# Halving the moving operand of one group of matmuls: the gate products of the second channel mixer in a two-layer decoder trunk

## The chip, the cores and the metric

One Trainium2 chip; the program runs on one core. The metric is device time in microseconds of one execution, as a median over runs. TensorE (PE, with its weight loads shown apart as PEld), VectorE (DVE), ScalarE (ACT), GpSimd (POOL) and SyncE (SP, which issues the large DMAs) run side by side and meet through semaphores.

## The reference

A decoder trunk of two layers over 256 tokens with a width of 2048. The first layer mixes tokens by sparse attention, the second by stick-breaking attention on a shared K/V; each is followed by a channel mixer, and every branch is normalised, shifted and scaled by a conditioning vector. What the change touches is the channel mixer of the second layer (`layer = 1`, `D_FF = 5632`):

```python
def swiglu(h, w_in, w_out):
    gate, up = jnp.split(h @ w_in, 2, axis=-1)
    return (jax.nn.silu(gate) * up) @ w_out

for layer in range(2):
    ...
    h = modulate(rms_norm(x, norm_g[layer, 2]), sh2, sc2)
    y = swiglu(h, ffn_w_in[layer], ffn_w_out[layer])
    x = x + g2[:, None, :] * rms_norm(y, norm_g[layer, 3])
```

All inputs are float32, and `h @ w_in` has 256 x 2048 by 2048 x 11264 elements; the left half of the result is the gate, the right half is up.

## The kernel before

**Tiling.** A weight matrix is cut into blocks of 512 columns (`nb`), and each block into four pieces of 512 rows (`kt`). One piece is one DMA of 1 MB into a page `raw` of 128 partitions x 2048 (four chunks `j` of 128 rows, 512 columns each). ScalarE rounds it into a page `wh` of type float32r, and VectorE subtracts to get the remainder `wl`. The activations are split in the same way into `hh` and `hl`; they lie transposed, in one page per `kt` (called `hhF` in the profile for the channel mixers). The 256 tokens are two tiles `t` of 128.

**The products.** For every chunk `j`, `piece` issues three matmuls into one PSUM bank `acc` of 128 x 512 float32: `hh` by `wh`, `hh` by `wl`, `hl` by `wh`. The 128 x 128 tile of activations is the stationary operand, and the 128 x 512 chunk of weights is the moving one, so that each matmul brings a weight load of its own (an LDWEIGHTS row in the profile, of the activations). The profile's names read out<-moving,stationary: `acc<-wh,hhF` is the first and the third of the three, `acc<-wl,hhF` the second.

**The channel mixer.** `ffn_units(l, key, ...)` has 11 blocks of 512 gate columns (segment `"g0"` in the first layer, `"g1"` in the second) and 11 of up columns (`"u0"`, `"u1"`), alternately: gate block, up block, next gate block. One block is 4 `kt` x 2 `t` x 4 `j` x 3 = 96 matmuls. After six blocks comes a part of the output product (`"p1"`), then the other five blocks, then the rest (`"y1"`). When a gate block is done, ScalarE takes its silu (`sg`), VectorE multiplies by up, and TensorE transposes the result (`aT`), between later products.

**What sets the order.** The whole program is written out by a planner (`Emit`) that runs while the program is built. It keeps a clock per engine and adds the cost that `_cost` gives each instruction; by these clocks it decides when a weight piece is split, which of the waiting side jobs (transposes, softmax, modulation vectors) comes between two products, which page or bank a tile gets, and how many filler matmuls (`idle<-identb`, bf16, 256 columns, results unused) `fill` puts ahead of a matmul that it expects to wait. A changed cost can therefore change the order. `_cost` gives a matmul with a float32r moving operand of `n` columns `n / 2400 + 0.0133` us. Besides the products above, the `gate_unit` of the first layer has 48 float32r matmuls of 256 columns (`gacc`, stationary `wh` or `wl` of 48 columns).

Every engine call goes through the helper `Engine.call`, so all instructions have its line in the profile: L118 before, L119 in the changed kernel.

Of the kernel before, what the change touches and what calls it, by code (L numbers as in the profile page):

```python
# [10 lines left out]
R32 = mybir.dt.float32r  # L11
# [14 lines left out]
NB = 512  # L26
# [33 lines left out]
FILL_LEAVE = 0.7  # L60
LEADS = (5.0, 5.0, 5.0)
M_FFN = 80

C_ID, C_NTRI, C_ANY, C_NEG1, C_ONE, C_KEEP = 0, 128, 256, 258, 259, 260
C_MASK, C_MASKT, C_CMP, C_COS, C_SIN, C_END = 260, 388, 516, 548, 804, 1060
# [32 lines left out]
class Engine:  # L98
# [5 lines left out]
    def __getattr__(self, op):  # L104
        f = getattr(self.real, op)
        E, eng = self.E, self.name

        def call(*a, **k):
            acc = k.get("accum_out")
            aps = [v for v in list(a) + [v for n, v in k.items() if n != "accum_out"] if hasattr(v, "free_size")]  # L110
            out, ins = aps[0], aps[1:]
            load = 0.0
            if eng == "ACT" and a[2] in TABLES and TABLES[a[2]] != E.table:
                E.table, load = TABLES[a[2]], 1.28
            if eng == "PE":
                E.fill(aps)
            E.enter(eng, _cost(eng, op, out, ins, k, acc), [out] + ([acc] if acc is not None else []), ins, load)
            return f(*a, **k)  # L118

        return call  # L120


def _cost(eng, op, out, ins, k, acc):
    n = out.free_size()
    if eng == "PE":
        if op == "transpose":
            return 0.109
        if ins[1].dtype != F32:
            return max(n / 2400.0 + 0.0133, 0.04)
        if out.shape[0] <= 64 and n >= 128:  # L130
            return n / 2400.0 + 0.09 if out.shape[0] <= 32 else n * 2 / 2400.0 + 0.02
        return 2 * max(n * 2 / 2400.0 + 0.0133, 0.109)
    n = max([n] + [i.free_size() for i in ins])
    if eng == "ACT":
        ptr = sum(hasattr(k.get(x), "free_size") for x in ("bias", "scale")) + (acc is not None)
        return 0.08 + n * 0.000833 + 0.093 * ptr
    if eng == "DMA2":
        return 3.0
    if eng == "DMA":
        return n * 4 * P / 383e3  # L140
    fast = op in ("tensor_scalar", "tensor_copy") and out.space == ins[0].space and list(ins[0].ap)[-1][0] == 1
    ptr = 0.055 * (op in ("tensor_scalar", "scalar_tensor_tensor"))
    return 0.075 + ptr + n / (1920.0 if fast else 960.0)
# [308 lines left out]
def kernel(ctx: ExitStack, tc, consts, x, c, mod_w, mod_b, norm_g, ffn_w_in, ffn_w_out, a_w_in,  # L452
# [9 lines left out]
    V, A, T, DMA = E.V, E.A, E.T, E.D  # L462
# [1142 lines left out]
    def mods_of(vecs):  # L1605
        return [("mod", v, k) for v in vecs for k in range(16)]
# [3 lines left out]
    def keys_of(a, b):  # L1610
        ks = []
        for u in units[a:b]:
            k = u.get("key")
            if k and k not in seen:
                seen.add(k)
                ks.append(k)
        return ks
# [4 lines left out]
    def spread(ks, mods, tail, head=0):  # L1622


        tot = sum(cost(k) for k in ks[head:len(ks) - tail])
        o, m, c = [], 0, 0.0
        for i, k in enumerate(ks):
            if i >= head:
                c += cost(k)
            want = min(len(mods), round(len(mods) * c / tot))  # L1630
            while m < want:
                o.append(mods[m])
                m += 1
            o.append(k)
        return o
# [22 lines left out]
    m1 = mods_of([(0, 5), (2, 1), (2, 0), (1, 1), (1, 0)])  # L1658
    order += spread(keys_of(n_l0, n_f0), m1[:M_FFN], TAIL, HEAD)
    order += spread(keys_of(n_f0, n_l1), m1[M_FFN:] + mods_of([(1, 2), (1, 4), (1, 3)]), TAIL, HEAD)  # L1660
    order += spread(keys_of(n_l1, len(units)), mods_of([(1, 5)]), 20, HEAD)
# [33 lines left out]
    def release(u, i):  # L1695
        if last_use[u["key"]] == i:
            del E.ready[u["key"]]
            E.put("pg")
            if u["key"][0] != "w1":
                E.put("pg")  # L1700
        if u["kind"] == "mm" and last_lhs[u["lhs"]] == i:
            E.put("pg")

    def weights(key):
        return E.ready[key][2] if key in E.ready else None

    def bank(tag):
        return E.when_free(tag)

    def latest(*ts):  # L1710
        return None if any(x is None for x in ts) else max(ts)

    def mm_unit(i, u):
        t, lhs = u["t"], u["lhs"]

        def start_time():
            return latest(weights(u["key"]), E.flags.get(u.get("flag", (lhs[0], lhs[1], t))),
                          bank(u["tag"]) if u["start"] else 0.0)

        js = u.get("js", range(4))  # L1720

        def piece(j):
            if u["start"] and j == 0:
                accs[u["acc"]] = E.alloc(u["tag"], "acc")
            wh, wl, _ = E.ready[u["key"]]
            o = accs[u["acc"]]
            hh = L[lhs][:, 0, j, t * P:(t + 1) * P]
            hl = L[lhs][:, 1, j, t * P:(t + 1) * P]
            T.matmul(o, hh, wh[:, j], start=u["start"] and j == 0, stop=False)
            T.matmul(o, hh, wl[:, j], start=False, stop=False)  # L1730
            T.matmul(o, hl, wh[:, j], start=False, stop=u["stop"] and j == 3)
            if j == js[-1]:
                if u["stop"]:
                    first = u["acc"][0] in ("g0", "g1", "kv") and u["nb"] == 0 and t == 0
                    E.spawn(after(u["epi"](accs.pop(u["acc"]), t, u["nb"]), E.fin + 0.1, first), front=True)
                release(u, i)

        return Unit(u["key"], start_time, [lambda j=j: piece(j) for j in js])

    def after(gen, t, calm=False):  # L1740
        yield t
        while calm and E.urgent:
            yield False
        yield from gen
# [73 lines left out]
```

## Time and profile before

| what | value |
|---|---|
| time, median of 3 runs | 2411.55 us (2410.32 to 2412.08) |
| the profiled execution, first to last instruction | 2407.8 us (its whole time is not listed; the median is 3.75 us above this) |
| mean granted TensorE clock | 0.996 |
| PE busy, PEld busy | 2356.9 us (98%), 1906.6 us (79%) |
| DVE busy, ACT busy | 1633.4 us (68%), 1077.6 us (45%) |
| HBM traffic | 272 GB/s over the span |

The busy time of PE is a union of intervals whose ends are modelled, and neighbouring matmuls overlap in the record; the distance between the starts of two matmuls tells more than the duration of one. In the rows of the timeline, equal neighbours are merged: the first number is the start, the second the length from the first start to the last end, and xN the count.

### The profile page before, as it was taken

Reading aid. Unit: us, or ns where it says so; the run is one execution under the profiler, and the core shown is the slowest. Engines: PE = TensorE matmul, PEld = TensorE weight load, DVE = VectorE, ACT = ScalarE, POOL = GpSimd, SP = SyncE. Lnnn points to the kernel's source line nnn. Section 1 sums busy time; section 2 is a strip of 40 time slices with the busy share of each in tenths; the row PEclk is TensorE's granted clock in tenths of the full one; section 3 lists DMA queues with packets and bytes.
Section 4 is the critical chain, followed back from the end, with each engine's and each line's share of the span. In section 5 each row is a group of like instructions: output and inputs, shape, how many; then the busy total and the mean of one; then the engine's idle time right before and its main releaser. Section 6 shows DMA issues by size and latency. Waiting matters only on the chain.

```text
span 2407.8 us, 27188 instructions
## 1 busy us (share of the span) xinstructions
PE 2356.9 (98%) x11124; PEld 1906.6 (79%) x11124; DVE 1633.4 (68%) x1346; ACT 1077.6 (45%) x1217; POOL 5.6 (0%) x14
## 2 busy tenths in 40 slices
PE   6999999999999999999999999999999999999998
PEld 4677777877888888888877788887888888888886
DVE  3788789978766667767768778865645454554554
ACT  4343455563433333333455455765433333333342
POOL 0000000000000000000000000000000000000000
PEclk9999999999999999999999999999999999999999
DMA  9998967979887699878758979845756547855642
GB/s 350 389 388 281 354 245 250 362 252 397 283 309 273 224 330 399 327 273 307 260 197 333 339 272 399 315 166 196 269 191 220 200 152 244 304 193 196 221 160 105
DMA packets 265629, 657.54 MB, mean 273 GB/s; under 512 B 12449, under 2 KB 30113, under 8 KB 240161
## 3 DMA queue, kind: packets, MB, share of 16 engines
q1 hardware_dynamic: 263808, 649.13, 75.0%
q0 software_dynamic: 992, 6.32, 0.7%
q8 instruction: 87, 1.43, 0.2%
q10 hardware_dynamic: 704, 0.36, 0.1%
q14 instruction: 38, 0.30, 0.0%
HBM read 653.64 MB, written 2.13 MB: 272 GB/s over the span
## 4 chain that ended last, share of the span: by engine, by line
PE 86%; ACT 4%; DMA 4%; DVE 3%; SPq 1%; issue 1%; ACTq 0%; DVEq 0%
PE acc L118 78%; DMA raw<-in_a_w_in_dram 2%; PE sc L118 1%; SPq L118 1%; DVE wl L118 1%; PE oT L118 1%; PE z L118 1%; ACT wh L118 1%; ACT hf L118 1%; ACT junk L118 1%; PE aT L118 1%; DMA modw<-in_mod_w_dram 1%; PE pmod L118 1%; DMA modq<-in_mod_w_dram 1%; PE hT L118 1%
## 5 line engine op out<-in xcount | busy, mean ns | idle before, releaser
L118 DVE TENSOR_TENSOR wl<-raw,wh 128x2048 fp32r<-128x2048 f32 (+2 forms) x392 | 880.0, 2249 | 516.9 <-ACT wh L118 477.8
L118 ACT ACTIVATE wh<-raw 128x2048 fp32r<-128x2048 f32 (+2 forms) x392 | 734.6, 1880 | 683.5 <-PE acc L118 478.7
L118 PE MATMUL acc<-wh,hhF 128*128 128x512 f32 x2816 | 883.7, 392 | 0.0
L118 PEld LDWEIGHTS acc<-wh,hhF 128*128 128x128 f32 x2816 | 530.4, 188 | 113.7 <-issue 4.2
L118 PE MATMUL acc<-wl,hhF 128*128 128x512 f32 x1408 | 549.3, 390 | 0.0
L118 DVE SCALAR_TENSOR_TENSOR macc<-modw,cact,macc 128x2048 f32<-128x2048 f32 x180 | 422.5, 2347 | 38.1 <-DMA modw<-in_mod_w_dram 29.2
L118 PE MATMUL acc<-wh,fa 128*128 128x512 f32 x1408 | 437.4, 390 | 0.0
L118 PEld LDWEIGHTS acc<-wh,fa 128*128 128x128 f32 x1408 | 264.3, 188 | 55.8 <-issue 0.8
L118 PEld LDWEIGHTS acc<-wl,hhF 128*128 128x128 f32 x1408 | 265.4, 188 | 53.8
L118 PE MATMUL acc<-wl,fa 128*128 128x512 f32 x704 | 273.9, 389 | 0.0
L118 PE MATMUL acc<-wh,hA 128*128 128x512 f32 x640 | 220.7, 404 | 1.4 <-DVE hA L118 0.7
L118 PE MATMUL acc<-wh,hhK 128*128 128x512 f32 x512 | 161.4, 392 | 0.9 <-ACT wh L118 0.7
L118 PEld LDWEIGHTS acc<-wl,fa 128*128 128x128 f32 x704 | 132.2, 188 | 26.9
L118 PEld LDWEIGHTS acc<-wh,hA 128*128 128x128 f32 x640 | 120.1, 188 | 39.7 <-issue 15.0
L118 PE MATMUL acc<-wl,hA 128*128 128x512 f32 x320 | 125.4, 392 | 3.0 <-DVE wl L118 3.0
L118 PEld LDWEIGHTS acc<-wh,hhK 128*128 128x128 f32 x512 | 96.0, 188 | 22.6 <-ACT wh L118 1.1
L118 PE MATMUL acc<-wl,hhK 128*128 128x512 f32 x256 | 100.3, 392 | 1.2 <-DVE wl L118 1.2
L118 ACT ACTIVATE fa<-aT 128x512 fp32r<-128x512 f32 x44 | 26.0, 594 | 162.8 <-PE aT L118 150.6
L118 PE MATMUL acc<-wh,hhB 128*128 128x512 f32 x256 | 87.5, 401 | 0.0
L118 PE MATMUL acc<-wh,oA 128*128 128x512 f32 x256 | 84.8, 398 | 0.0
L118 PE MATMUL acc<-wh,oB 128*128 128x512 f32 x256 | 82.4, 394 | 0.0
L118 PEld LDWEIGHTS acc<-wl,hA 128*128 128x128 f32 x320 | 60.4, 189 | 13.6 <-DVE wl L118 4.2
(183 smaller groups left out, 1664.9 us busy)
## 6 DMA issues: line engine op xcount, KB each, us to landing
raw<-in_ffn_w_in_dram SPq DMA_DIRECT2D x176, 1024.0 KB, 5.3
modw<-in_mod_w_dram SPq DMA_DIRECT2D x160, 1024.0 KB, 7.1
raw<-in_ffn_w_out_dram SPq DMA_DIRECT2D x88, 1024.0 KB, 5.3
raw<-in_a_w_in_dram SPq DMA_DIRECT2D x40, 1024.0 KB, 14.2
modq<-in_mod_w_dram SPq DMA_DIRECT2D x32, 1024.0 KB, 14.1
modw<-in_kv_mod_w_dram SPq DMA_DIRECT2D x32, 1024.0 KB, 5.7
raw<-in_kv_w_dram SPq DMA_DIRECT2D x32, 1024.0 KB, 7.6
raw<-in_a_w_out_dram SPq DMA_DIRECT2D x16, 1024.0 KB, 7.1
```

Source lines behind the costliest of these rows:

```text
L118: return f(*a, **k)
```

## The change

In `piece`, the gate products of the second layer (`"g1"` alone) are issued as two matmuls of 256 columns each instead of one of 512, for each of the three products. Both halves have the same stationary tile and go to the two halves of the same bank. The accumulation of the bank is started by the first half alone. The planner's cost of a float32r matmul of exactly 256 columns becomes `256 * 17 / 16 / 2400` = 0.1133 us, from 0.1200 us; a matmul of 512 columns stays at 0.2266 us. This cost also holds for the 48 `gacc` matmuls of the first layer, whose form is not changed.

```diff
+HALVES = ("g1",)
...
         if ins[1].dtype != F32:
+            if ins[1].dtype == R32 and n == NB // 2:
+                return n * 17 / 16 / 2400.0
             return max(n / 2400.0 + 0.0133, 0.04)
...
-            T.matmul(o, hh, wh[:, j], start=u["start"] and j == 0, stop=False)
-            T.matmul(o, hh, wl[:, j], start=False, stop=False)
-            T.matmul(o, hl, wh[:, j], start=False, stop=u["stop"] and j == 3)
+            n_h = 2 if u["acc"][0] in HALVES else 1
+            for p, (st_, mv) in enumerate(((hh, wh), (hh, wl), (hl, wh))):
+                for i2 in range(n_h):
+                    cs = slice(i2 * NB // n_h, (i2 + 1) * NB // n_h)
+                    T.matmul(o[:, cs], st_, mv[:, j, cs], start=u["start"] and j == 0 and p == 0 and i2 == 0,
+                             stop=u["stop"] and j == 3 and p == 2, skip_group_check=n_h > 1)
```

On TensorE, the start of the first gate block of the second layer reads before (a row is out<-moving,stationary, its output shape and the count of equal neighbours; `acc` is the block's bank, `hhF` the activations):

```order
L118 MATMUL acc_11522<-wl_11452,oB_11130 128x512
L118 MATMUL acc_11522<-wh_11451,oB_11130 128x512
L118 MATMUL acc_11666<-wh_11470,hhF_1779_11605 128x512
L118 MATMUL acc_11666<-wl_11471,hhF_1779_11605 128x512
L118 MATMUL acc_11666<-wh_11470,hhF_1779_11605 128x512 x2
```

And the same place on TensorE after (the first two rows are the end of the attention's output product, `oB`):

```order
L119 MATMUL acc_11528<-wl_11458,oB_11136 128x512
L119 MATMUL acc_11528<-wh_11457,oB_11136 128x512
L119 MATMUL acc_11672<-wh_11476,hhF_1780_11611 128x256 x2
L119 MATMUL acc_11672<-wl_11477,hhF_1780_11611 128x256 x2
L119 MATMUL acc_11672<-wh_11476,hhF_1780_11611 128x256 x4
```

Every `hhF` matmul has become two of half the width, in the same place; what stands between the blocks (`aT` and the rest) stands where it stood.

The other place where TensorE's rows differ is in the first layer, between the compressed blocks' products (`hid<-rawd,xpe`) and the small products that follow them (`hid<-L,hid`), where TensorE waits for ScalarE to copy `hid`. Before:

```order
L118 MATMUL hid_1852<-rawd_1714,xpe_1401 64x256 x8
L118 MATMUL hid_1852<-rawd_1752,xpe_1401 64x256 x8
L118 MATMUL hid_1852<-L_3_81,hid_1905 128x64 x2
L118 LDWEIGHTS identb
L118 MATMUL idle_1914<-identb 128x256
```

The same rows of TensorE after:

```order
L119 MATMUL hid_1852<-rawd_1681,xpe_1401 64x256 x8
L119 MATMUL hid_1852<-rawd_1714,xpe_1401 64x256 x8
L119 MATMUL hid_1852<-rawd_1752,xpe_1401 64x256 x8
L119 LDWEIGHTS identb
L119 MATMUL idle_1908<-identb 128x256
```

Five fillers have come in ahead of the wait; the five that followed it are still there. On VectorE, ScalarE, GpSimd and SyncE all instructions stand in the order they had; fourteen of them, in the last third of the program, wait for other semaphores, since pages go round in another way.

## The prediction

> **What bounds the kernel now.** I first read the page: the busy line, the chain that ended last and the granted clock.
>
> ```profile
> PE 2356.9 (98%) x11124; PEld 1906.6 (79%) x11124; DVE 1633.4 (68%) x1346; ACT 1077.6 (45%) x1217; POOL 5.6 (0%) x14
> PE 86%; ACT 4%; DMA 4%; DVE 3%; SPq 1%; issue 1%; ACTq 0%; DVEq 0%
> PEclk9999999999999999999999999999999999999999
> ```
>
> TensorE is the bound, at full clock, and each of its 11124 matmuls has one weight load: no load is saved when two neighbours have the same stationary tile. Next the stretch in which the changed matmuls lie, and their groups.
>
> ```profile
> 1711.00:2230.00 519.00, 519.00 (x2324) 429.62 (x2324) 264.37 (x142) 200.68 (x137) 0.00 (x0) 1.00 0.62 213
> L118 PE MATMUL acc<-wh,hhF 128*128 128x512 f32 x2816 | 883.7, 392 | 0.0
> L118 PE MATMUL acc<-wl,hhF 128*128 128x512 f32 x1408 | 549.3, 390 | 0.0
> ```
>
> The first row (PE, PEld, DVE, ACT, POOL busy, clock, DMA) shows PE busy for all of 519 us, with VectorE at 264 and ScalarE at 201: both have slack, and whatever TensorE's matmuls take there goes straight into the end time. The group rows end in an idle time of 0.0. They hold both layers, gate and up: 2816 + 1408 = 4224 matmuls, of which the second layer's gate is a quarter, 1056. So 1056 matmuls of 512 columns become 2112 of 256, with 2112 weight loads.
>
> The mean of 390 ns is a latency; what counts is the distance between starts. The timeline of TensorE in a gate block, and of its weight loads at the same place:
>
> ```profile
> 1725.31 0.39 PE L118 MATMUL acc<-wl,hhF 128*128 128x512 f32 x1
> 1725.54 0.62 PE L118 MATMUL acc<-wh,hhF 128*128 128x512 f32 x2
> ...
> 1728.71 0.39 PE L118 MATMUL acc<-wl,hhF 128*128 128x512 f32 x1
> ```
> ```profile
> 1725.32 0.41 PEld L118 LDWEIGHTS acc<-wh,hhF 128*128 128x128 f32 x2
> 1725.77 0.19 PEld L118 LDWEIGHTS acc<-wl,hhF 128*128 128x128 f32 x1
> ```
>
> From 1725.31 to 1728.71 lie 15 matmuls (five times wl, wh, wh): 3.40 / 15 = 226.7 ns each. The load for the next matmul starts when a matmul starts (1725.32 against 1725.31), is recorded for 0.19 us, and is over before the next start. So a matmul waits for the longer of two things: the stream of the one before it, and the load that began with that one.
>
> **The change, term by term.**
>
> *Stream of a half.* The nearest row is the gate product of the first layer, the only float32r matmul here with 256 moving columns:
>
> ```profile
> 242.13 0.28 PE L118 MATMUL gacc<-hA,wl 128*48 128x256 f32 x1
> 242.24 0.39 PE L118 MATMUL gacc<-hA,wh 128*48 128x256 f32 x2
> ...
> 243.83 0.28 PE L118 MATMUL gacc<-hA,wl 128*48 128x256 f32 x1
> ```
>
> Again 15 matmuls lie between the ends: 1.70 / 15 = 113.3 ns. That is half of 226.7, so the time goes with the columns and I see no fixed part per instruction. Two halves: 2 x 113.3 - 226.7 = 0. The lower bound is the pace of the bf16 fillers of 256 columns:
>
> ```profile
> 42.95 2.24 PE L118 MATMUL idle<-identb 128*128 128x256 bf16 x19
> L118 PE MATMUL idle<-identb x86: 272/273/309, 26.8 to 1576.3; 128*128 128x256 bf16 x86
> ```
>
> (2.24 - 0.273) / 18 = 109.3 ns, which would give 2112 x (109.3 - 113.3) = -8.4 us. It is another type, so I take gacc's 0 and keep -8.4 as the bound.
>
> The Trainium skill, "TensorE: Matmul & The Clock Gate", section "Back-to-back issue gap", gives N / 2.4 + 2.5 ns for a matmul of N columns, hence a fixed 2.5 ns that each additional instruction pays again. By that rule two halves would cost 2.5 ns more than one whole, in sum an estimated 1056 x 2.5 = 2.6 us. Its 215.8 and 109.2 ns do not agree with the 226.7 and 113.3 of these float32r rows, which show no such part, so the measurement decides.
>
> *Load of a half.* gacc's stationary tile has only 48 columns, so it does not show a 128-column load within 113.3 ns. Where matmuls are so short that loads alone set the pace, the profile does: 15 moving columns, 128 stationary ones.
>
> ```profile
> 263.30 0.86 PEld L118 LDWEIGHTS cs<-L,qT 128*128 128x128 f32 x7
> L118 PEld LDWEIGHTS cs<-L,qT x64: 187/192/192, 263.1 to 406.6; 128*128 128x128 f32 x64
> ```
>
> (0.86 - 0.192) / 6 = 111.3 ns from load to load, though one is recorded for 192: a load's recorded length is no occupancy. In float32r the two loads of a pair in the stick-breaking stage, and the two that follow, start 0.11 apart:
>
> ```profile
> 1533.84 0.19 PEld L118 LDWEIGHTS acc<-wh,hhB 128*128 128x128 f32 x1
> 1533.95 0.19 PEld L118 LDWEIGHTS acc<-wl,hhB 128*128 128x128 f32 x1
> ```
>
> So the load needs 111.3 and the stream 113.3, and the stream still sets the pace, with 2 ns to spare (in the whole matmuls it had 115). Term: 0. It is the term I trust least, since each ns beyond the margin costs 2112 x 0.001 = 2.1 us. Its upper bound is the one place where 512 float32r columns go as two matmuls, 384 and 128, each with its load:
>
> ```profile
> 1533.04 0.45 PE L118 MATMUL z<-el,tri 128*128 128x384 f32 x2
> 1533.32 0.45 PE L118 MATMUL z<-eh,tri 128*128 128x384 f32 x2
> 1533.61 0.45 PE L118 MATMUL z<-el,tri 128*128 128x384 f32 x2
> 1533.89 0.45 PE L118 MATMUL acc<-wh,hhB 128*128 128x512 f32 x1
> ```
>
> 0.85 / 3 = 283 ns per pair, 57 more than 226.7: as a price, 1056 x 57 = +60 us. But the two rules above explain it: 384 columns stream in 384 x 113.3 / 256 = 170 ns, and the 128 columns, 57 ns by the same rate, are shorter than the load behind them and take its 111 to 113; 170 + 113 = 283. Halves of 256 are both just longer than a load. I therefore stay at 0 and keep +60 as the far bound.
>
> *Starts of a block.* The blocks are interrupted by transposes and the like, and the built program has 22 unbroken runs of halves. After an interruption gacc was slower for a few matmuls:
>
> ```profile
> 239.66 0.28 PE L118 MATMUL gacc<-hA,wl 128*48 128x256 f32 x1
> 240.13 0.39 PE L118 MATMUL gacc<-hA,wh 128*48 128x256 f32 x2
> ```
>
> Four matmuls in 0.47, 117.5 ns each, 4.2 above the pace, 17 ns in all. 22 x 17 ns = 0.4 us if whole matmuls paid nothing there. I take +0.4, bounds 0 and 0.4.
>
> *Fillers.* Five more fillers of 109.3 ns, 0.55 us, stand ahead of the wait for ScalarE in the first layer:
>
> ```profile
> 253.01 1.91 ACT L118 ACTIVATE wh<-raw 128x2048 fp32r<-128x2048 f32 x1 [8.40 <-DMA raw<-in_a_w_in_dram]
> 254.82 0.75 ACT L118 ACTIVATE hid<-hid 64x256 f32<-64x256 f32 x2
> 255.63 0.66 PE L118 MATMUL hid<-L,hid 128*128 128x64 f32 x4 [3.96 <-ACT hid L118]
> 256.60:260.10 3.50, 3.15 (x17) 2.05 (x15) 2.90 (x2) 1.84 (x3) 0.00 (x0) 0.51 1.05 386
> ```
>
> The wait of 3.96 us is set by a DMA that ScalarE awaits first, so 0.55 us are hidden; if the wait were gone they would cost 0.55. The last row shows the clock at 0.51 for 3.5 us right after that wait. If the fillers keep the clock up, half of that, 1.7 us, is gained; they run at the start of the wait, some 3.4 us before its end, so I take 0 and bounds of -1.7 and +0.55.
>
> *Other waits.* ScalarE, VectorE and SyncE keep their order. Fourteen rows wait for other semaphores because pages go round differently; ScalarE already waits for pages that TensorE holds:
>
> ```profile
> ACT wh L118 <- PE acc L118: 174.4, 56, 9.0
> ```
>
> (1678 to 2290 us: total, times, longest), and no wait of TensorE stands against these in that stretch. With the same pace of TensorE these covers stay; term 0. If the halves became slower, the pages would come free later, but only as late as TensorE itself is.
>
> Sum: 0 + 0 + 0.4 + 0 + 0 = +0.4 us on the profiled span of 2407.8. The median of the runs, 2411.55, is 3.75 above that span, and I add the sum to it: 2412.0 us.
>
> **The rivals.**
>
> *The load loses its margin.* Place: each of the 2112 loads; it decides when the pace passes 115.6 ns, since 0.2% of the time is 4.8 us and 4.8 / 2112 = 2.3 ns. (Differences under 0.2% are about what a measurement here cannot tell from none.) For it: only 2 ns of margin, and gacc's 117.5 after an interruption, which an interlock without slack may never make up. At that pace 2112 x 4.2 = +8.9 us: 2420.4, slower. Against it: the 111.3 already holds the whole round from load to matmul to next load.
>
> *Two short matmuls cost as the 384 and 128 pair does:* +60 us, 2472. Against it, the working above.
>
> *The load is occupied for its recorded 188 ns or so.* Then a half takes some 190 ns: 2112 x (190 - 113.3) = +162 us, 2574. The Trainium skill, "Perfetto Trace Analysis", section "Identifying the Most-Contended Engine", has TensorE judged by the busy share of its weight loads; by it, the stretch above would go from 429.62 / 519 = 83% to beyond full. Against it: cs starts loads every 111.3 ns that are recorded for 192.
>
> *Faster.* Halves at the bf16 pace give -8.4 us, 2403; for it speaks only another type's row.
>
> **Chances and range.** No change 0.75; lost margin 0.12; the pair's price 0.05; recorded length 0.03; faster 0.05. Hence faster 0.05, same 0.75, slower 0.20. The likeliest case alone, with the clock's 1.7 us and the spread of the runs, lies within 2408.5 to 2414. For 8 in 10 I reach to the lost margin at 2420.4 and a little beyond: 2408 to 2422, which leaves out the two dear cases and most of the fast one.
>
> **What would show it.** In the changed profile: acc rows of 256 columns, 2112 in all, 15 of them in 1.70 us; a load at each start; PE still without idle time between 1711 and 2230; the up blocks unchanged at 226.7; wait and clock near 256 us as before. The prediction is wrong if steady halves lie more than 115.6 ns apart (the load), or if time appears outside the gate blocks.

## The result: 13 us slower, and all of it in the pace of the halves

| | median us | runs | ratio to before, 95% interval |
|---|---|---|---|
| before | 2411.55 | 3 (2410.32 to 2412.08) | |
| changed | 2424.82 | 3 (2423.85 to 2424.89) | 1.0056 [1.0036, 1.0076] |

The forecast was 2412.0 us, within 2408 to 2422. The kernel became 13.3 us slower.

TensorE in a gate block of the changed kernel, and its weight loads at the same place (timeline: start, length of the merged row, count):

```profile
1725.35 0.40 PE L119 MATMUL acc<-wl,hhF 128*128 128x256 f32 x2
1725.59 0.64 PE L119 MATMUL acc<-wh,hhF 128*128 128x256 f32 x4
...
1727.51 0.40 PE L119 MATMUL acc<-wl,hhF 128*128 128x256 f32 x2
```
```profile
1725.23 0.31 PEld L119 LDWEIGHTS acc<-wl,hhF 128*128 128x128 f32 x2
```

From 1725.35 to 1727.51 lie 18 halves (three times two wl and four wh): 2.16 / 18 = 120.0 ns each, where 113.3 was forecast. Two halves take 240.0 ns in place of 226.7, and 1056 x 13.3 = 14.1 us. The loads still overlap: two in 0.31 us, recorded for 0.19 each.

The stretch with the last ten gate and ten up blocks, before and after (PE, PEld, DVE, ACT, POOL busy, clock, DMA share, GB/s):

```profile
1712.35:2289.13 576.78, 576.78 (x2589) 476.48 (x2588) 293.50 (x159) 222.27 (x153) 0.00 (x0) 1.00 0.62 213
```
```profile
1715.33:2304.47 589.14, 589.14 (x3548) 527.05 (x3547) 293.67 (x159) 222.13 (x153) 0.00 (x0) 1.00 0.61 209
```

PE is busy throughout in both, the clock is full, and VectorE and ScalarE do the same work. 959 more matmuls cost 12.36 us, 12.9 ns each. So nothing waits that did not wait before: TensorE itself takes longer. The first gate and up block lie ahead of this stretch:

```profile
1662.44:1712.35 49.91, 47.78 (x214) 39.37 (x212) 34.47 (x41) 28.86 (x45) 0.00 (x0) 0.97 0.71 253
```
```profile
1662.60:1715.33 52.73, 51.04 (x324) 45.83 (x323) 36.84 (x47) 31.31 (x52) 0.00 (x0) 1.00 0.73 258
```

The first halved block begins at 1665.83 in the changed kernel, 3.2 us into the second row's window, so the pair of blocks takes 49.50 us against 49.91. Before, the granted clock was lower here (0.97 over the window, 0.79 from 1673 to 1681 us, which at half the clock is 3.4 us); in the changed kernel's profile it was not. That is worth an estimated 1.7 us, half of the 3.4, and hides the pair's own 1.3. That it comes from the halves is not shown: of the runs below in which this first gate block is whole, three have the drop (0.86 over 1672 to 1684 us) and three do not (1.00). From the first gate block to the last up block the sum is +12.0 us.

The profiled span grew by 15.3 us; the other 3.4 lie before the stage. There the changed kernel's profile has the lower clock (0.99 and 0.89 over 0 to 240 and 240 to 270 us, before 1.00 and 0.94). The run of the planner's cost alone, next, has the same fillers and is as fast as the kernel before, so the fillers are not the reason. That the spans differ by 15.3 and the medians by 13.3 is spread: a run takes 1.8 us more than its span (2424.89 against 2423.1), so the profiled execution of before, with its span of 2407.8, took an estimated 2409.6, 2 us under the median.

### The profile page after: what moved, and what is told of

It is laid out like the page before. It is cut to its first block, busy times and chain, and to the rows that moved or that the text cites. A ratio compares the mean times of both kernels' runs of the same rounds, so it can differ in the third digit from the quotient of the medians.

```text
span 2423.1 us, 29321 instructions
## 1 busy us (share of the span) xinstructions
PE 2371.9 (98%) x12185; PEld 1963.8 (81%) x12185; DVE 1633.7 (67%) x1346; ACT 1077.5 (44%) x1217; POOL 5.6 (0%) x14
## 4 chain that ended last, share of the span: by engine, by line
PE 88%; ACT 4%; DVE 3%; DMA 3%; issue 1%; SPq 1%; ACTq 0%; DVEq 0%
PE acc L119 81%; PE sc L119 1%; PE oT L119 1%; DMA raw<-in_a_w_in_dram 1%; PE z L119 1%; DVE wl L119 1%; ACT wh L119 1%; SPq L119 1%; ACT junk L119 1%; PE aT L119 1%; ACT hf L119 1%; DMA modw<-in_mod_w_dram 1%; PE pmod L119 1%; DMA modq<-in_mod_w_dram 1%; PE hT L119 1%
## 5 line engine op out<-in xcount | busy, mean ns | idle before, releaser
L119 PE MATMUL acc<-wh,hhF 128*128 128x512 f32 (+1 forms) x3520 | 892.3, 349 | 0.2 <-ACT hhF L119 0.2
L119 PEld LDWEIGHTS acc<-wh,hhF 128*128 128x128 f32 x3520 | 593.4, 190 | 87.3 <-issue 4.2
L119 PE MATMUL acc<-wl,hhF 128*128 128x512 f32 (+1 forms) x1760 | 554.0, 347 | 0.0
L119 PEld LDWEIGHTS acc<-wl,hhF 128*128 128x128 f32 x1760 | 308.8, 190 | 39.8
```

## The experiments

Two theories of the 120 ns were set against each other. **F**: each float32r matmul of N columns with a load of 128 columns pays a fixed 13.3 ns beyond N / 2.4 ns; a whole of 512 has always paid it (213.3 + 13.3 = 226.7), and halves pay it twice. (F is the planner's cost in the kernel before, `n / 2400 + 0.0133` us.) **L**: the stream goes with the columns (17/16 of N / 2.4), and a dense chain of float32r loads goes round in 120 ns.

**The planner's cost alone**, and **the halves alone**:

```diff
-HALVES = ("g1",)
+HALVES = ()
```

> No product is halved; only the planner's new cost of a 256-column float32r matmul is kept, and with it the five fillers and the other round of pages. If all of the added time is in the halves (theories F and L below), this runs as the kernel before, 2411.55 us within 2 us. If the fillers or the changed waits cost something, it is several us slower, up to the 13 us of the whole change.

Measured: 2410.44 us against 2410.34, ratio 1.0001 [0.9992, 1.0010]. The fillers, the new cost and the other round of pages cost nothing that this comparison can show; its interval is some 2 us to either side.

```diff
-            if ins[1].dtype == R32 and n == NB // 2:
-                return n * 17 / 16 / 2400.0
```

> The gate products are halved, the planner's costs are the old ones, so that a half is planned at 0.1200 us and the fillers stay as before. Both theories put the added time into the halves: 2112 x (120.0 - 113.3) = 14.1 us, so 2424 to 2427 us. If the planner's cost was part of the trouble, it is nearer to 2412.

Measured: 2423.39 against 2410.34, ratio 1.0056 [1.0042, 1.0070]. That is 13.1 us more, just below the expected 2424 to 2427. The effect is in the halves; a part of the plan in it, if any, is below what these intervals show.

**Pace against columns.** All but a bank's first matmul stream only the first `nc_` columns past `m_` stationary ones, another pair in each gate block. (The rest of the products is left out, and the total times of these runs mean nothing.)

```diff
+            nc_, m_ = FORMS.get(u["nb"], (NB, P)) if u["acc"][0] == "g1" else (NB, P)
...
+                n_, r_ = (NB, P) if first_ else (nc_, m_)
+                T.matmul(o[0:r_, 0:n_], st_[:, 0:r_], mv[:, j, 0:n_], start=first_,
...
```

> In the gate blocks 1 to 10 of the second layer all matmuls but the first of a bank stream only 448, 384, 320, 288, 256, 224, 192, 160, 128 and 64 columns of the 512 (the rest of those products is left out), all with a stationary tile of 128 columns; the plan is as before. Read is the distance of steady starts. Theory F (a fixed 13.3 ns with each load of 128 columns, on top of N / 2.4 ns): 200.0, 173.3, 146.7, 133.3, 120.0, then the floor of a load, 111 to 112, for the rest. Theory L (the stream costs N x 17/16 / 2.4 ns, and a dense chain of float32r loads goes round in 120 ns): 198.3, 170.0, 141.7, 127.5, 120, and 120 for all the rest. The rows at 320 and 288 columns (5 and 6 ns apart) and those at 192 and below (8 ns apart) tell them apart.

The timeline of TensorE in the blocks of 384, 320 and 128 columns:

```profile
1762.09 0.33 PE L120 MATMUL acc<-wl,hhF 128*128 128x384 f32 x1
...
1765.21 0.33 PE L120 MATMUL acc<-wl,hhF 128*128 128x384 f32 x1
...
1801.57 0.31 PE L120 MATMUL acc<-wl,hhF 128*128 128x320 f32 x1
...
1802.89 0.31 PE L120 MATMUL acc<-wl,hhF 128*128 128x320 f32 x1
...
2167.16 0.28 PE L120 MATMUL acc<-wl,hhF 128*128 128x128 f32 x1
...
2169.84 0.28 PE L120 MATMUL acc<-wl,hhF 128*128 128x128 f32 x1
```

Between the ends of each pair lie 18, 9 and 24 matmuls: 3.12 / 18 = 173.3, 1.32 / 9 = 146.7 and 2.68 / 24 = 111.7 ns. L had 170.0, 141.7 and 120: it falls, in the wide rows and in the floor. F had 173.3, 146.7 and 111 to 112. (At 448 columns, 205.6 ns, both were too low.) At 320 columns the matmuls start 35 ns further apart than the 111.7 in which loads go round at 128 columns, and the 13.3 are paid all the same. A load that comes late is therefore not their cause, unless a load beside a wider stream takes longer than that, which no run here shows.

> Finer steps with 128 stationary columns: blocks 1 to 10 stream 496, 480, 464, 432, 416, 352, 272, 248, 240 and 264 columns (the rest is left out). A constant fixed part gives (N + 32) / 2.4 ns: 220.0, 213.3, 206.7, 193.3, 186.7, 160.0, 126.7, 116.7, 113.3, 123.3. If starts lie on a grid of 16 columns (6.67 ns), 248 goes at 120.0 and 264 at 126.7. If 448's 206.7 was no slip but a second law for wide matmuls, 432 to 496 lie 6.7 ns or more above these values.

Paces from both runs (mean distance of starts in one block each, gaps over 1.3 times the median left out), and what they are above N / 2.4:

| columns | 512 | 496 | 480 | 464 | 448 | 432 | 416 | 384 | 352 | 320 | 288 | 272 | 264 | 256 | 248 |
|---|---|---|---|---|---|---|---|---|---|---|---|---|---|---|---|
| ns | 227.1 | 222.9 | 216.8 | 209.1 | 205.6 | 195.6 | 186.9 | 173.8 | 162.0 | 146.7 | 131.7 | 125.5 | 120.2 | 119.5 | 114.3 |
| above | 13.8 | 16.2 | 16.8 | 15.8 | 18.9 | 15.6 | 13.6 | 13.8 | 15.3 | 13.4 | 11.7 | 12.2 | 10.2 | 12.8 | 11.0 |

At 240 columns and fewer, down to 128, the floor of 111 to 112 takes over (64 columns follow below). The grid as expected is not there (248 is below 120, 264 below 126.7); that starts are rounded the other way is not ruled out, since 264 goes at the pace of 256. The part above the columns is 10 to 19 ns, not one constant; the expectation of exactly 13.3 was too sharp, and the second law for wide matmuls only half fits (3 ns above it at 464 to 496, not 7). The part is 14 to 19 ns at 416 columns and more and 10 to 13 at 248 to 288, so it falls somewhat, but a part that went with the columns would halve.

The gaps left out hide something. In every profile the granted clock is 0.50 for short stretches, and one of them lies in the block of 352 columns (windows row as above, then TensorE):

```profile
2073.64:2077.06 3.42, 3.42 (x14) 3.42 (x13) 1.14 (x1) 1.61 (x2) 0.00 (x0) 0.50 0.53 162
```
```profile
2074.62 0.49 PE L120 MATMUL acc<-wl,hhF 128*128 128x352 f32 x1
...
2076.38 0.49 PE L120 MATMUL acc<-wl,hhF 128*128 128x352 f32 x1
```

Six matmuls in 1.76 us are 293.3 ns, where twice the 162.0 of the full clock would be 324. Whole products of 512 columns go at 426.7 at the half clock (in the run past 64 columns, below, three lie between 2168.03 and 2169.31 us); twice 226.7 would be 453. Both are N / 1.2 with nothing added: in these rows the column part is N / 2.4 at the full clock, and the fixed part is there at the full clock alone. The block of 64 columns is mostly at the half clock (0.50 from 2206 to 2220 us), and its starts lie 213 ns apart there, 112 where the clock was full.

**Pace against stationary columns.**

> As in the run on columns, but with smaller stationary tiles (the products of the other tokens are left out): blocks 1 to 4 stream 512 columns past 96, 64, 48 and 32 stationary ones, blocks 5 to 9 stream 256 past 112, 96, 64, 48 and 32, block 10 streams 384 past 64. Theory F, with the fixed part going with the loaded columns (13.3 ns for 128, 6.7 for 64 or fewer by the first layer's gate product): 512 columns at 223, 220, 218 to 220, 217 to 220 ns; 256 at 118, 117, 113, 113, 110 to 113; 384 at 166.7. Theory L: all of the 512 at 226.7, 384 at 170, and 256 at 113.3 for all, since a load of 112 columns or fewer goes round in less than 113.3.

512 columns past 64 stationary ones, and 256 past 64:

```profile
1763.86 0.39 PE L120 MATMUL acc<-wl,hhF 128*64 128x512 f32 x1
...
1768.69 0.39 PE L120 MATMUL acc<-wl,hhF 128*64 128x512 f32 x1
...
2109.49 0.28 PE L120 MATMUL acc<-wl,hhF 128*64 128x256 f32 x1
...
2110.86 0.28 PE L120 MATMUL acc<-wl,hhF 128*64 128x256 f32 x1
```

21 matmuls in 4.83 us are 230.0 ns, 12 in 1.37 are 114.2. So neither theory's account of the load holds: a smaller load saves nothing at 512 (230.0, 230.0, 233.2, 231.5 ns past 96, 64, 48, 32, all above the 226.7 past 128) nor at 384 (173.7 past 64), but it saves 3 to 6 ns at 256 (116.6, 116.7, 113.9, 117.2, 115.9 past 112, 96, 64, 48, 32).

> As the run on columns, with a stationary tile of 64 columns: blocks 1 to 10 of the second layer's gate stream 448, 384, 320, 288, 256, 224, 192, 160, 128, 96 columns (the other products are left out). The run on stationary columns had 113.3 ns at 256 and about 173 at 384. If the fixed part belongs to the matmul and not to its load (theory F), the paces are those of 128 stationary columns, (N + 32) / 2.4 ns: 200, 173, 147, 133, 120, 107, 93, 80, 67, 53, with a lower floor, near 60, for the shorter load. If it belongs to the load running beside the stream (theory G), they are at most (N + 16) / 2.4: 193, 167, 140, 127, 113, 100, 87, 73, 60.

Measured: 202.3, 173.3, 145.0, 130.3, 113.7, 103.3, 88.6 and 73.5 ns from 448 down to 160 columns, which is 15.6, 13.3, 11.7, 10.3, 7.0, 10.0, 8.6 and 6.8 above N / 2.4. At 128 and 96 columns the clock was full in one part of the block and 0.50 in the other (1.00 from 2161 to 2164 us, 0.50 from 2165 to 2170): starts lie 57 to 60 ns apart in the one, near the floor expected for the shorter load, and 107 in the other. Past 64 columns the part shrinks with narrower matmuls and lies between F and the G of the expectation, except at 448, where it is above both. The first layer's gate product, 256 columns past 48, goes at 113.3; the same sizes in the run on stationary columns went at 117.2, and 256 past 64 at 113.7 and 113.9. Its 113.3 was read rightly, and was not the price of 256 past 128.

**Doubling the dose, and a third split.**

```diff
-HALVES = ("g1",)
+HALVES = ("g1", "u1")
```

> The up products of the second layer are halved too: 2112 chunks in place of 1056. Theory F: 2112 x (240.0 - 226.7) = 28.2 us over whole products, a ratio of 1.0117 to the kernel before. If the price came from something that is paid once per stage (blocks' starts, pages), it stays near 13 us.

Measured: 2435.86 against 2411.05, +24.8 us, ratio 1.0102 [1.0085, 1.0119]. The last ten pairs of blocks in its profile:

```profile
1714.44:2315.97 601.53, 601.53 (x4510) 577.91 (x4508) 293.57 (x159) 222.11 (x153) 0.00 (x0) 1.00 0.59 205
```

(601.53 - 576.78) / (4510 - 2589) = 12.9 ns per additional matmul, as with half the dose. The interval takes in 28.2 us.

```diff
-            n_h = 2 if u["acc"][0] in HALVES else 1
+            cuts = (0, 384, NB) if u["acc"][0] in HALVES else (0, NB)
```

> The second layer's gate products go as 384 and 128 columns instead of two halves; everything is computed. Theory F with the floor of a load: 173.3 + 112 = 285 ns per chunk instead of 226.7, 1056 x 58.6 = 62 us, a ratio of 1.0257 to the kernel before. A fixed part alone, with no floor (173.3 + 66.7 = 240): the same 14 us as the halves.

Measured: 2471.38 against 2411.05, +60.3 us, ratio 1.0251 [1.0236, 1.0266]. The timeline of TensorE in one of its gate blocks:

```profile
1739.99 0.45 PE L119 MATMUL acc<-wl,hhF 128*128 128x384 f32 x2
...
1743.43 0.45 PE L119 MATMUL acc<-wl,hhF 128*128 128x384 f32 x2
```

12 chunks in 3.44 us are 286.7 ns; expected were 285. The floor of the load, from the prediction, and the fixed part together give the price of a split to within 2 us.

**Another type.** bf16 matmuls on constants stand between or in place of float32r ones, as further forms of the same sampling:

```diff
+                for q, what in enumerate(("r512",) if first_ else form):
...
+                        T.matmul(o[:, 0:n_], identb, identb.unsqueeze(1).to_broadcast([P, n_ // P, P]),
...
```

> In some gate blocks of the second layer bf16 matmuls on constants (stationary 128 x 128, results unused) stand between or in place of the float32r ones; part of the products is left out. Block 1 alternates float32r and bf16 of 256 columns, block 2 float32r of 512 and bf16 of 256, block 3 has bf16 of 512 alone, block 4 bf16 of 256 alone, block 5 alternates float32r and bf16 of 512, block 7 has two float32r of 256 and one bf16 of 256. If the fixed part belongs to each float32r matmul whatever follows it (theory F), block 1 goes in pairs of 120 + 109 = 229 ns, block 2 in 227 + 109 = 336, block 7 in 349. If it is paid only where float32r follows float32r with a load under way (theory G), the pairs take 106.7 + 109 and a little = 216 to 220 and 322 to 326, block 7 takes 336 to 340. Blocks 3 and 4 should show the bf16 paces, near 216 and 109.

The blocks of bf16 alone, in the timeline of TensorE, and the bf16 loads where float32r and bf16 of 256 alternate:

```profile
1822.54 2.75 PE L120 MATMUL acc<-identb 128*128 128x512 bf16 x12
...
1865.03 7.70 PE L120 MATMUL acc<-identb 128*128 128x256 bf16 x69
```
```profile
1722.07 0.10 PEld L120 LDWEIGHTS <-identb 128*128 128x128 bf16 x1
...
1723.05 0.10 PEld L120 LDWEIGHTS <-identb 128*128 128x128 bf16 x1
```

With one matmul's 0.38 and 0.28 taken off, (2.75 - 0.38) / 11 = 215.5 and (7.70 - 0.28) / 68 = 109.1 ns: a fixed part of 2.1 to 2.4 ns beyond N / 2.4, a fifth of float32r's. The alternating pairs answer nothing: from 1722.07 to 1723.05 lie four, 245 ns each, above both expectations (229, and 216 to 220), and so are the others (358 and 360 where F had 336 and 349). A bf16 load starts only 5 ns before its matmul there, and the next float32r matmul starts 39 ns after that; a change of type seems to bring a price of its own, which no run takes apart. Nor does any run separate the matmul from its load, since each has one. What the float32r part is made of, and why it is gone at the half clock, stays open.

## Why the prediction was wrong

- **Stream of a half**: this step failed. It took 113.3 ns from gacc and concluded that there is "no fixed part per instruction". The term is 2112 x (120.0 - 113.3) = 14.1 us, not 0. Two points, 512 past 128 and 256 past 48, differed in two things (and gacc moves activations past weights), and the ratio of exactly one half was chance: past 128 stationary columns 256 take 120.0. The right price stood in the kernel: the planner's old cost, 256 / 2400 + 0.0133 = 0.1200 us, is the pace that the halves took, and the change replaced it by 0.1133.
- The rule of the Trainium skill ("TensorE: Matmul & The Clock Gate", "Back-to-back issue gap") that each additional matmul pays a fixed part again was set aside there, and was right in kind. Its 2.5 ns agrees with the bf16 rows (109.1 at 256); float32r paid some 13.3 at the full clock.
- **Load of a half**: right. The round of 111.3 ns came back as the floor of 111 to 112 at 240 columns and fewer, and the +60 us named as the price of a 384 and 128 split was measured as +60.3.
- **The load loses its margin** (2420.4 us): its sign, a pace beyond 115.6 ns, came, and its time was near, but its reason holds at most in part. At 288 to 384 columns a load of 111 to 112 ns has 20 ns and more to spare, and 12 to 15 ns are paid all the same. A smaller load saves 1 to 2 ns at 288 and 320 and 3 to 6 at 256; what share the load has at 256 stays open.
- **Starts of a block**: forecast at +0.4 us. The halves cost 12.9 ns per matmul over ten blocks where their steady pace alone gives 13.3, so over these blocks the interruptions cost an estimated 0.4 us less than with whole matmuls, not more.
- **Fillers and other waits**: 0 forecast, a ratio of 1.0001 measured. The clock near 256 us was not as before (0.89 against 0.94 over 240 to 270 us), but not through the fillers: it was 0.94 with the fillers alone and 0.89 with the halves alone. PE without idle time and the full clock in the gate blocks came as forecast; the median pace of the up blocks stayed at 227.
- **The clock** at the first gate block was not in the forecast: the drop that was there before is missing in the changed kernel's profile, and in those of the other runs with halves or a split. As it is missing in some profiles with a whole first block too, the 1.7 us that it seems to give back are not shown to come from the change.

## What to carry to other kernels

A pace from another shape carries over only if the moving and the stationary size both match; where one row misses, look for rows that vary one of them alone, and leave the range open to a fixed part per instruction as large as the excess of the wide matmul over its columns (here 13.3 ns of 226.7). Keep float32r matmuls as wide as the bank: at the full clock each cut costs about 13 ns here, and a piece under some 240 columns costs a whole load round of 111 ns. Shrinking the stationary tile does not buy the fixed part back at 512 columns.

## What was not expected of the hardware

- At the full clock float32r pays 10 to 19 ns per matmul beyond its columns past 128 stationary ones, and bf16 2.1 to 2.4 ns with a load of the same shape. At a granted clock of 0.50 float32r pays nothing: 293.3 ns at 352 columns, 426.7 at 512.
- 448 columns (205.6 ns) are worse than their neighbours 464 and 432 by some 3 ns above the columns, in one block of one execution.
- Alternating float32r and bf16 matmuls of 256 cost 245 ns a pair, 16 more than 120 and 109 apart.
